# A two-layer hybrid decoder trunk: 28 of 32 tiles of the first feed-forward product, in pairs, by seven products of half blocks in place of eight

## The chip, the cores and the metric

One core of one Trainium2 chip runs the whole program. The metric is device time in microseconds (us): 1336.36 us, the median of three runs (1335.64 to 1336.46).

## The reference, cut to what matters

Two layers over 512 tokens of width 1024, all in fp32. Each layer has one input projection, four token mixers beside each other (a gated delta rule, latent attention, HGRN2, dilated attention), one output projection, and a feed-forward block, with a layer norm behind each half:

```
for l in range(2):
    h = x @ w_in[l]                                   # 1024 -> about 3100
    mixed = concat(A(h), B(h), C(h), D(h)) @ w_out[l]
    x = layer_norm(alpha * x + mixed, ln1_g[l], ln1_b[l])
    x = layer_norm(alpha * x + square(relu(x @ w_ff1[l])) @ w_ff2[l], ln2_g[l], ln2_b[l])
```

The product `x @ w_ff1[l]` is 512 by 1024 by 4096, and `... @ w_ff2[l]` is 512 by 4096 by 1024.

## The kernel before, in words

Every large product is made of three matmuls in the fp32r type: an operand is split into a high part (the value rounded to fp32r, written by ScalarE) and a low part (the value less its high part, written by VectorE), and `mm3` adds high by high, high by low and low by high in PSUM. For a weight tile of 128 by 1024 the raw tile is `wr` (loaded by a DMA that SyncE issues, two buffers), its parts are `wh` and `wl` (five buffers each). `weights` loads and splits, `split` is the pair of instructions. The stream x stands transposed, as `xH` and `xL`, eight blocks of 128 channels by 512 tokens.

The first feed-forward product goes tile by tile. A tile is 128 of the 4096 outputs: `proj` runs eight channel blocks by three matmuls, 24 matmuls of 512 columns, into one PSUM buffer; then ScalarE writes relu into `h2` and VectorE multiplies it by the PSUM value, which squares it. The first four tiles run as two halves of 256 columns (tokens 256 to 511 first), so that they can begin while the layer norm still makes the other tokens; the other 28 are full width. The second product then takes the 32 tiles `h2` as its weights side: each is split into `hH` and `hL`, and 24 matmuls of 512 columns per tile add into eight PSUM buffers.

`layer_norm(0, ...)` ends the first half of a layer: it normalises four blocks of 128 tokens without scale and bias into `xt`, transposes them on TensorE, and applies scale and bias on the way out of PSUM (`lny`), from which `xH` and `xL` are split. The residual needs the same values untransposed: before, `flush` loads scale and bias as tables (`ln`), multiplies and adds (16 VectorE instructions) early in the first feed-forward product, and writes the result to memory (`mid`); `load_x` fetches it 12 tiles before the end of the second product.

The order is not that of the text. Each instruction is recorded with its dependencies (class `Plan`), and `order` chooses at build time, by table costs, which goes next on which engine; `BIAS`, `FILL`, `EMA` and the counts of buffers steer it. Each engine then works strictly in the order that came out. Nearly every instruction passes through the one line that calls the engine (L522 before, L523 in the changed file), so rows are told apart by the tile's name. Rows from the trace drop buffer numbers, and write `h` for `h2`.

Of the kernel before, what the change touches and what calls it, by code (L numbers as in the profile page):

```python
# [9 lines left out]
FT = mybir.dt.float32  # L10
FR = mybir.dt.float32r
I32 = mybir.dt.int32
AF = mybir.ActivationFunctionType
OP = mybir.AluOpType
# [13 lines left out]
           "cf0", "cf1", "cq0", "cq1", "ci0", "ci1", "cg0", "cg1",  # L28
           "bq", "bkv", "dk0", "dk1", "dq0", "dq1", "dva", "dvb"]
ROWS = 41  # L30
BIGS = 5
RESERVE = {"row": 0, "ps": 0}
FIFO = ("wr", "wh", "wl")
FILL = (0.1, 0.4)
EMA = 3000.0
BURST = 4
PATIENCE = 1000.0
DENSE = 0.8
BIAS = {('', 've'): -550, ('A', 'ac'): 400, ('A', 'po'): 1400, ('A', 've'): -25, ('A0', 'ac'): -250,
# [4 lines left out]
GROUPS = ((2, 3), (4, 5), (0, 1, 6, 7))  # L44
WBIAS = 0
OBIAS = 400
# [117 lines left out]
class Plan:  # L164
# [48 lines left out]
    def cost(self, e, method, out, ins, k):  # L213
        n = math.prod(out.shape[1:])
        psum = any(v.buf.kind == "ps" for v in [out, *ins])
        if e == "pe":
            if method == "transpose":
                return 109.0
            w, x = k["lhsT"], k["rhs"]
            n, m = math.prod(x.shape[1:]), w.shape[1]  # L220
            if w.dt == FR:
                return max(n * 0.4167 + 13.5, 109.0)
            t = 2 * max(2 * n * 0.4167 + 3, 2 * min(m, n) * 0.4167 + 3, 25.0)
            return t
        if e == "ve":
            if method == "transpose":
                wide = len(out.shape) > 2 and out.shape[1] == 8
                return 446.0 if wide else 1045.0
            if method in ("tensor_scalar", "tensor_copy") and not psum:
                return 64 + 0.52 * n  # L230
            if method == "memset":
                return 30.0
            if method == "reciprocal":
                return 68 + 6.3 * n
            if method == "scalar_tensor_tensor" and not psum and n > 64:
                return 95 + 1.1 * n
            if method == "tensor_tensor_reduce":
                return 195 + 1.045 * n
            return 67 + 1.045 * n
        if e == "ac":  # L240
            if method == "dma_start":
                return 60.0
            ap = sum(not isinstance(k.get(w, 0.0), (int, float)) for w in ("bias", "scale"))
            acc = 90.0 if k.get("accum_out") is not None else 0.0
            return (51 if psum else 93) + (60 * ap if n <= 128 and psum else 93 * ap) + acc + 0.833 * n
        if e == "po":
            if method == "tensor_scalar":
                return 150 + 4.2 * n
            return 190 + 2.2 * n
        return 450.0  # L250
# [274 lines left out]
def emit(ctx, tc, io, layers=DEPTH):  # L525
# [18 lines left out]
    def ps(tag, shape=(128, 512), name=None):  # L544
        return plan.tile("ps", list(shape), FT, tag, "mm" if tag == "mm" else None)
# [42 lines left out]
    xH = const("xH", [128, KT, S], FR)  # L588
    xL = const("xL", [128, KT, S], FR)
    xt = None  # L590
    undone, undone_tables = [], []
    xsrc = io["x"]

    def split(h, lo, src):
        ac.activation(h, src, AF.Copy)
        ve.tensor_tensor(lo, src, h.bitcast(FT), OP.subtract)

    def weights(src, bias=WBIAS, n=1024, kind="wr"):
        plan.bias = -bias
        raw = plan.tile(kind, [128, 1024], FT, "wr")[:, :n]  # L600
        sy.dma_start(raw, src)
        h = plan.tile("wh", [128, 1024], FR, "wh")[:, :n]
        lo = plan.tile("wl", [128, 1024], FR, "wl")[:, :n]
        split(h, lo, raw)
        plan.bias = 0
        return h, lo
# [6 lines left out]
    def proj(w, out, cols=slice(0, S)):  # L613
        for k in range(KT):
            ks = slice(128 * k, 128 * k + 128)
            mm3(out[:, cols], (w[0][:, ks], w[1][:, ks]), (xH[:, k, cols], xL[:, k, cols]), k == 0, k == KT - 1)
# [52 lines left out]
    for l in range(layers):  # L669
        pcol = lambda i, r=slice(0, 128): par[r, l, i:i + 1]  # L670
        wcol = lambda n: weights(io["w_in"][l, W_AT[n]])

        mixH, mixL = [None] * KT, [None] * KT
        mid = plan.tile("dram", [NT, 128, D], FT, "x1")

        def gated(ot, gate, gain, k, tag):
            sq = row("gsq")
            ac.activation(sq, ot, AF.Square)
            s = ps(tag)
            total(s, bdr, [sq])  # L680
            rsqrt(sq, s, 1.0 / 64)
            ve.scalar_tensor_tensor(sq, sq, pcol(gain), gate, op0=OP.mult, op1=OP.mult)
            m = row("gm")
            ve.tensor_tensor(m, ot, sq, OP.mult)
            mixH[k], mixL[k] = row(f"mixH{k}", FR), row(f"mixL{k}", FR)
            split(mixH[k], mixL[k], m)

        def norm_tables(i, gate, l=l):
            g = []
# [8 lines left out]
        def layer_norm(i, m, acc, scale, after, gb_=None):  # L698
# [23 lines left out]
            for c in range(2):  # L722
                cs = slice(512 * c, 512 * c + 512)
                if last:
                    ve.scalar_tensor_tensor(t[c], t[c], s[:, 5:6], gb_[1][c], op0=OP.mult, op1=OP.add)
                    sy.dma_start(after[m, :, cs], t[c])
                    continue
                ve.tensor_scalar(t[c], t[c], s[:, 2:3], s[:, 5:6], op0=OP.add, op1=OP.mult)
                o = ps("a", (128, 4, 128))
                y = row("lny")  # L730
                for j in range(4):
                    k = 4 * c + j
                    pe.transpose(o[:, j], t[c][:, 128 * j:128 * j + 128], ident)
                for j in range(4):
                    k, js = 4 * c + j, slice(128 * j, 128 * j + 128)
                    g, b = pcol(P_LN + 16 * i + k), pcol(P_LN + 16 * i + 8 + k)
                    if j in LN_ACT:
                        ac.activation(y[:, js], o[:, j], AF.Identity, bias=b, scale=g)
                    else:
                        ve.tensor_scalar(y[:, js], o[:, j], g, b, op0=OP.mult, op1=OP.add)  # L740
                ks, ms = slice(4 * c, 4 * c + 4), slice(128 * m, 128 * m + 128)
                split(xH[:, ks, ms], xL[:, ks, ms], v3(y, 4))
            if not last:
                undone.append((t, after[m]))

        def tables_of(i, f=norm_tables):
            undone_tables.append(lambda gate: f(i, gate))
# [11 lines left out]
            undone.clear()  # L759

        def load_x(gate):
            nonlocal xt
            xt = [[row("xt") for c in range(2)] for m in range(NT)]
            for m in range(NT):
                for c in range(2):
                    sy.dma_start(xt[m][c], xsrc[m, :, 512 * c:512 * c + 512], after=gate)

        def w_tile(ks, ws, m, first, last=False):
            ms, acc = slice(128 * m, 128 * m + 128), []
# [543 lines left out]
        plan.stream = "O"  # L1313
        for g in GROUPS:
            w_out(g, g is GROUPS[0], g is GROUPS[-1])
        tables_of(0)


        plan.stream = "F"

        h2 = []
        for f0 in range(0, MF, 4):
            ws = [weights(io["w_ff1"][l, f0 + i]) for i in range(4)] if f0 == 0 else None
            if f0 == 0:
                accs = [ps(t) for t in ("mm", "mm", "a", "b")]
                for cols in (slice(256, 512), slice(0, 256)):
                    for i in range(4):
                        proj(ws[i], accs[i], cols)
            if f0 == 4:
                flush()  # L1330
            for i in range(4):
                if f0 == 0:
                    o = accs[i]
                else:
                    w = weights(io["w_ff1"][l, f0 + i])
                    o = ps("mm")
                    proj(w, o)
                t = row("h2")
                ac.activation(t, o, AF.Relu)
                ve.tensor_tensor(t, t, o, OP.mult)  # L1340
                h2.append(t)
        acc = [[ps("a"), ps("a")], [ps("a"), ps("b")], [ps("b"), ps("b")], [ps("mm"), ps("mm")]]
        TAIL = 4

# [7 lines left out]
        tail, gb_ = [], None  # L1352
        xsrc = mid
        for k in range(MF):
            if k == MF - 12:
                load_x(plan.mark())
                if l == layers - 1:
                    gb_ = norm_tables(1, plan.mark())
            w = weights(io["w_ff2"][l, k])
            hk = (row("hH", FR), row("hL", FR))  # L1360
            split(hk[0], hk[1], h2[k])
            if k < MF - TAIL:
                for m in range(NT):
                    ff2(m, k, hk, w)
            else:
                tail.append((k, hk, w))
# [135 lines left out]
```

## Time and profile before

| | |
|---|---|
| median of three runs | 1336.36 us |
| profiled execution, its own time | 1334.89 us |
| span of its instructions | 1333.1 us |
| TensorE matmuls busy | 1305.4 us, 98% |
| VectorE busy | 741.6 us, 56% |
| ScalarE busy | 620.8 us, 47% |
| mean granted TensorE clock | 0.996 |
| first feed-forward product, full-width tiles | 333.4 to 490.2 us, 994.6 to 1151.4 us |
| second feed-forward product | from 490.2 us, and from 1151.4 us |

A span is the time from the first instruction to the last. The profiled execution took 1.8 us more than its span, and 1.5 us less than the median of the runs. Matmuls overlap in the engine's pipeline, so the recorded length of one is longer than the distance from its start to the next start; for a run of them the chain of waits gives the true pace.

### The profile page before, as it was taken

To read this page: it belongs to the slowest core of one execution; us is meant where nothing else is said; L and a number is where in the kernel's file an instruction comes from. 1 tells how busy PE (TensorE), PEld (TensorE's weight loads), DVE (VectorE), ACT (ScalarE), POOL (GpSimd) and SP (SyncE) were. 2 spreads that over 40 slices of the span, in tenths; PEclk is the share of its full clock that TensorE was granted. 3 is DMA by queue.
4 is the path that set the end of the run, shared out by engine and by line. 5 is a ranking of instruction groups with operands and counts; after the bars stand their busy time and mean duration, and the time that the engine had idled before them with its cause. 6 is when DMAs were issued, how large, how long until landed. Compare 5 with 4: busy or idle time off the path is not lost.

```text
span 1333.1 us, 21834 instructions
## 1 busy us (share of the span) xinstructions
PE 1305.4 (98%) x8920; PEld 1060.9 (80%) x8920; DVE 741.6 (56%) x1505; ACT 620.8 (47%) x1194; POOL 4.8 (0%) x12
## 2 busy tenths in 40 slices
PE   8999999999999999999999999999999999999997
PEld 7767778779888888888887677787898888888886
DVE  6895575666733334422479977766766333343226
ACT  6854567737322223321587545766463222333222
POOL 0000000000000000000000000000000000000000
PEclk9999999999999999999999999999999999999999
DMA  6312102323533233334132241122145323333441
GB/s 226 124 59 65 59 18 79 109 83 95 189 109 92 94 88 100 104 104 149 48 111 96 79 144 50 34 96 96 64 124 192 91 91 95 91 98 106 145 124 63
DMA packets 44163, 132.65 MB, mean 100 GB/s; under 512 B 4896, under 2 KB 5152, under 8 KB 44064
## 3 DMA queue, kind: packets, MB, share of 16 engines
q1 hardware_dynamic: 44064, 131.27, 31.3%
q8 instruction: 70, 1.15, 0.3%
q14 instruction: 29, 0.24, 0.1%
HBM read 122.86 MB, written 8.39 MB: 98 GB/s over the span
## 4 chain that ended last, share of the span: by engine, by line
PE 82%; DVE 8%; ACT 7%; issue 1%; DMA 1%; DVEq 0%; SPq 0%; ACTq 0%
PE mm L522 47%; PE a L522 19%; PE b L522 15%; ACT lny L522 2%; DVE xt L522 2%; PE o L522 1%; ACT wh L522 1%; DVE wl L522 1%; DVE U L522 1%; ACT scr L522 1%; ACT xH L522 1%; DVE T L522 1%; DMA ln<-in_ln_dram 0%; DVE sn L522 0%; ACT kt L522 0%
## 5 line engine op out<-in xcount | busy, mean ns | idle before, releaser
L522 DVE TENSOR_TENSOR wl<-wr,wh 128x1024 fp32r<-128x1024 f32 (+1 forms) x195 | 236.7, 1218 | 340.5 <-ACT wh L522 338.0
L522 ACT ACTIVATE wh<-wr 128x1024 fp32r<-128x1024 f32 (+1 forms) x195 | 204.7, 1053 | 410.3 <-PE mm L522 391.6
L522 PE MATMUL mm<-xH,wh 128*128 128x512 f32 (+1 forms) x832 | 328.0, 394 | 0.1
L522 PE MATMUL mm<-xH,wl 128*128 128x512 f32 (+1 forms) x832 | 326.2, 393 | 0.0
L522 PE MATMUL mm<-xL,wh 128*128 128x512 f32 (+1 forms) x832 | 323.4, 389 | 0.0
L522 PEld LDWEIGHTS mm<-xH,wl 128*128 128x128 f32 x832 | 156.4, 188 | 36.9 <-issue 2.9
L522 PEld LDWEIGHTS mm<-xH,wh 128*128 128x128 f32 x832 | 156.3, 188 | 34.1 <-issue 2.3
L522 PEld LDWEIGHTS mm<-xL,wh 128*128 128x128 f32 x832 | 156.2, 188 | 33.8 <-issue 1.5
L522 DVE TENSOR_TENSOR hL<-h,hH 128x512 fp32r<-128x512 f32 x64 | 43.9, 692 | 73.3 <-PE mm L522 70.6
L522 ACT ACTIVATE hH<-h 128x512 fp32r<-128x512 f32 x64 | 40.5, 632 | 93.4 <-PE mm L522 73.7
L522 PE MATMUL b<-wh,hH 128*128 128x512 f32 x192 | 74.9, 390 | 0.0
L522 PE MATMUL b<-wh,hL 128*128 128x512 f32 x192 | 74.7, 389 | 0.0
L522 PE MATMUL a<-wh,hL 128*128 128x512 f32 x192 | 74.7, 389 | 0.0
L522 PE MATMUL a<-wl,hH 128*128 128x512 f32 x192 | 74.7, 389 | 0.0
L522 PE MATMUL a<-wh,hH 128*128 128x512 f32 x192 | 74.7, 389 | 0.0
L522 PE MATMUL b<-wl,hH 128*128 128x512 f32 x192 | 74.7, 389 | 0.0
L522 PE MATMUL mm<-wh,hH 128*128 128x512 f32 x128 | 49.9, 390 | 0.0
L522 PE MATMUL mm<-wh,hL 128*128 128x512 f32 x128 | 49.8, 389 | 0.0
L522 PE MATMUL mm<-wl,hH 128*128 128x512 f32 x128 | 49.8, 389 | 0.0
L522 ACT ACTIVATE at<-at,as 128x512 f32<-128x512 f32 (+3 forms) x64 | 35.7, 559 | 21.4 <-DVE as L522 21.3
L522 DVE TENSOR_TENSOR h<-h,mm 128x512 f32<-128x512 f32 x60 | 40.9, 682 | 5.6 <-ACT h L522 5.6
L522 PEld LDWEIGHTS a<-wh,hH 128*128 128x128 f32 x192 | 36.0, 188 | 7.6
(303 smaller groups left out, 2140.1 us busy)
## 6 DMA issues: line engine op xcount, KB each, us to landing
wr<-in_w_ff_dram SPq DMA_DIRECT2D x128, 512.0 KB, 3.6
wr<-in_w_in_dram SPq DMA_DIRECT2D x47, 512.0 KB, 3.7
wr<-in_w_out_dram SPq DMA_DIRECT2D x16, 512.0 KB, 3.6
x<-xt SPq DMA_DIRECT2D x24, 256.0 KB, 2.1
xt<-x SPq DMA_DIRECT2D x24, 256.0 KB, 5.5
ln<-in_ln_dram SPq DMA_DIRECT2D x16, 256.0 KB, 5.7
x<-in_xT_dram SPq DMA_DIRECT2D x8, 256.0 KB, 5.9
dtab<-in_tabs_dram SPq DMA_DIRECT2D x8, 256.0 KB, 4.5
```

Of the source, the lines that this page charges most:

```text
L522: getattr(e.real, method)(*[real(v) for v in a], **{n: real(v) for n, v in k.items()})
```

## The change

The 28 full-width tiles become 14 pairs of tiles. Write the channels as two halves (near, far) and the tokens as two halves (early: 256 to 511, late: 0 to 255). A pair of output tiles is then a two-by-two product of blocks, which takes eight block products, or, by Winograd's form of Strassen's scheme, seven block products and a number of additions of blocks. One block product (`part`) is four channel blocks by three matmuls of 256 columns, 12 matmuls.

Three of the seven products need combinations of x (`xd`, made once in a layer from the four pairs of `lny` that `normed` keeps; a fourth combination overwrites `xH` and `xL` of the near channels and late tokens), and three need combinations of the two raw weight tiles (`wd`, made for each pair). The products are then combined out of PSUM (`u`, `v`) into the two `h2` tiles, and relu and square are two ScalarE instructions. The first four tiles stay plain.

Beside that, the scale and bias of the first norm are no longer applied in `flush` during the first product. The normalised `xt` goes to memory as it is, and `load_x` loads two wide tables and does the 16 multiplications and additions on VectorE, late in the second product. The last norm's tables become two wide loads, there is one more `big` buffer, and the planner's numbers differ.

```diff
-BIGS = 5
+LOAD = 12
+BIGS = 6
+PLAIN = 4
-FILL = (0.1, 0.4)
-EMA = 3000.0
+FILL = (0.1, 0.2)
+EMA = 2000.0
-BIAS = {('', 've'): -550, ('A', 'ac'): 400, ('A', 'po'): 1400, ('A', 've'): -25, ('A0', 'ac'): -250,
...
+BIAS = {('A', 'ac'): 425, ('A0', 'ac'): -600, ('A0', 've'): 25, ('A1', 'ac'): 225, ('A1', 'pe'): -1775,
...
+        def wide_tables(i, gate, l=l):
+            g = []
+            for t in range(2):
+                b = big("ln", (128, 2, 512))
...
                 ve.tensor_scalar(t[c], t[c], s[:, 2:3], s[:, 5:6], op0=OP.add, op1=OP.mult)
+                if not i:
+                    sy.dma_start(after[m, :, cs], t[c])
...
+            if pending is not None:
+                g, pending = pending(gate), None
+                for m in range(NT):
+                    for c in range(2):
+                        ve.tensor_tensor(xt[m][c], xt[m][c], g[0][c], OP.mult)
+                        ve.tensor_tensor(xt[m][c], xt[m][c], g[1][c], OP.add)
...
-            if f0 == 4:
-                flush()
-            for i in range(4):
-                if f0 == 0:
-                    o = accs[i]
-                else:
-                    w = weights(io["w_ff1"][l, f0 + i])
-                    o = ps("mm")
-                    proj(w, o)
-                t = row("h2")
-                ac.activation(t, o, AF.Relu)
-                ve.tensor_tensor(t, t, o, OP.mult)
-                h2.append(t)
...
+        xd = [[plan.tile("big", [128, 4, 256], FR, "xd") for _ in range(2)] for _ in range(3)]
+        xd.append([xH[:, near, late], xL[:, near, late]])
+        for j in range(2):
+            t = [row("t") for _ in range(4)]
+            ve.tensor_tensor(t[0], normed[j, 0], normed[2 + j, 0], OP.subtract)
+            ve.tensor_tensor(t[1], normed[j, 1], t[0], OP.subtract)
+            ve.tensor_tensor(t[2], normed[j, 1], normed[j, 0], OP.subtract)
+            ve.tensor_tensor(t[3], normed[2 + j, 1], t[1], OP.subtract)
+            js = slice(128 * j, 128 * j + 128)
+            for (h, lo_), d in zip(xd, t):
+                split(h[:, :, js], lo_[:, :, js], v3(d, 4))
+
+        def part(w, c, x):
+            o = ps("mm", (128, 256))
+            for k in range(4):
+                ks = slice(c + 128 * k, c + 128 * k + 128)
+                mm3(o, (w[0][:, ks], w[1][:, ks]), (x[0][:, k], x[1][:, k]), k == 0, k == 3)
+            return o
...
+        for f0 in range(PLAIN, MF, 2):
+            r0, r1 = raw(f0), raw(f0 + 1)
+            w1, wd1, wd2 = hl(), hl(), hl()
+            w22 = row("w22", FR), row("w22", FR)
...
+            split(*w1, r0)
+            wd = [row("wd") for _ in range(4)]
+            ve.tensor_tensor(wd[0], r1[:, a], r1[:, b], OP.add)
+            split(wd1[0][:, a], wd1[1][:, a], wd[0])
+            ve.tensor_tensor(wd[1], wd[0], r0[:, a], OP.subtract)
+            split(wd1[0][:, b], wd1[1][:, b], wd[1])
+            ve.tensor_tensor(wd[2], r0[:, a], r1[:, a], OP.subtract)
+            split(wd2[0][:, a], wd2[1][:, a], wd[2])
+            ve.tensor_tensor(wd[3], r0[:, b], wd[1], OP.subtract)
+            split(wd2[0][:, b], wd2[1][:, b], wd[3])
+            split(*w22, r1[:, b])
...
+            o = part(w1, 0, x11)
+            ac.activation(u[:, 0], o, AF.Copy)
+            o = part(wd1, 512, xd[1])
+            ve.tensor_tensor(u[:, 1], u[:, 0], o, OP.add)
+            o = part(w1, 512, x21)
+            ve.tensor_tensor(t0[:, early], u[:, 0], o, OP.add)
+            o = part(wd1, 0, xd[0])
+            ve.tensor_tensor(v, u[:, 1], o, OP.add)
+            o = part(wd2, 0, xd[2])
+            ve.tensor_tensor(t1[:, late], v, o, OP.add)
+            ve.tensor_tensor(t1[:, early], u[:, 1], o, OP.add)
+            o = part(wd2, 512, x22)
+            ve.tensor_tensor(t0[:, late], v, o, OP.add)
+            ac.activation(t0, t0, AF.Relu)
+            ac.activation(t0, t0, AF.Square)
+            o = part(w22, 0, xd[3])
+            ve.tensor_tensor(t1[:, early], t1[:, early], o, OP.add)
+            ac.activation(t1, t1, AF.Relu)
+            ac.activation(t1, t1, AF.Square)
```

First place: VectorE in the middle of the first product, layer 0. Before, a low part of a weight tile (`wl`) and a square (`h2`) take turns:

```order
L522 TENSOR_TENSOR wl_4456<-wr_4397,wh_4446 128x1024
L522 TENSOR_TENSOR h2_4454<-h2_4454,mm_4414 128x512
L522 TENSOR_TENSOR wl_4490<-wr_4431,wh_4480 128x1024
L522 TENSOR_TENSOR h2_4488<-h2_4488,mm_4448 128x512
L522 TENSOR_TENSOR wl_4524<-wr_4465,wh_4514 128x1024
L522 TENSOR_TENSOR h2_4522<-h2_4522,mm_4482 128x512
```

Now, on VectorE again, 12 of the 17 instructions of a pair (the pair of the raw tiles `wr_4589` and `wr_4608`; `wl_4655`, `wl_4696` and `wl_4723` are low parts of its weights, `mm_4612`, `mm_4643` and `mm_4663` products of the pair ahead of it):

```order
L523 TENSOR_TENSOR h2_4646<-u_4593,mm_4612 128x256
L523 TENSOR_TENSOR wl_4655<-wr_4589,wh_4640 128x1024
L523 TENSOR_TENSOR h2_4614<-v_4636,mm_4643 128x256
L523 TENSOR_TENSOR wd_4673<-wr_4608 128x512
L523 TENSOR_TENSOR wd_4682<-wr_4589,wr_4608 128x512
L523 TENSOR_TENSOR h2_4646<-h2_4646,mm_4663 128x256
L523 TENSOR_TENSOR wl_4696<-wd_4673,wh_4685 128x512
L523 TENSOR_TENSOR wd_4705<-wd_4673,wr_4589 128x512
L523 TENSOR_TENSOR w22_4714<-wr_4608,w22_4661 128x512
L523 TENSOR_TENSOR wl_4723<-wd_4682,wh_4708 128x512
L523 TENSOR_TENSOR wd_4735<-wr_4589,wd_4705 128x512
L523 TENSOR_TENSOR wl_4696<-wd_4705,wh_4685 128x512
```

Four instructions for two tiles have become 17, and those that take a product out of PSUM stand between those that prepare the next pair's weights.

Second place: TensorE, the same stage. Before, a tile runs through its 24 matmuls without a change of the output:

```order
L522 MATMUL mm_4482<-xH_106,wh_4344 128x512
L522 MATMUL mm_4482<-xL_110,wh_4344 128x512
L522 MATMUL mm_4482<-xH_106,wl_4354 128x512
L522 MATMUL mm_4482<-xH_106,wh_4344 128x512
L522 MATMUL mm_4482<-xL_110,wh_4344 128x512
L522 MATMUL mm_4482<-xH_106,wl_4354 128x512
```

Now, on TensorE, the part of that pair in which the second half of `wl_4696` is used (`mm_4725` and `mm_4738` need the two halves of `wd1`, `mm_4751` the first half of `wd2`):

```order
L523 MATMUL mm_4738<-xd_3756,wh_4685 128x256
L523 MATMUL mm_4738<-xd_3794,wh_4685 128x256
L523 MATMUL mm_4725<-xd_3744,wh_4685 128x256
L523 MATMUL mm_4725<-xd_3783,wh_4685 128x256
L523 MATMUL mm_4725<-xd_3744,wl_4696 128x256
L523 MATMUL mm_4725<-xd_3744,wh_4685 128x256
L523 MATMUL mm_4725<-xd_3783,wh_4685 128x256
L523 MATMUL mm_4725<-xd_3744,wl_4696 128x256
L523 MATMUL mm_4751<-xd_3764,wh_4708 128x256
L523 MATMUL mm_4751<-xd_3803,wh_4708 128x256
L523 MATMUL mm_4751<-xd_3764,wl_4723 128x256
L523 MATMUL mm_4738<-xd_3756,wl_4696 128x256
```

The product `mm_4738` is begun, left for nine matmuls of two others, and then goes on with its first matmul that needs the low part; in all a pair is 84 matmuls of 256 columns.

Third place: VectorE and the first norm's tables. Before, at the first full-width tiles of the first product:

```order
L522 TENSOR_TENSOR wl_3968<-wr_3905,wh_3960 128x1024
L522 TENSOR_TENSOR hL_3983<-h2_3951,hH_3972 128x512
L522 TENSOR_TENSOR xt_3311<-xt_3311,ln_3970 128x512
L522 TENSOR_TENSOR xt_3302<-xt_3302,ln_3970 128x512
L522 TENSOR_TENSOR xt_3315<-xt_3315,ln_3976 128x512
```

Now, on VectorE, between the weight tiles of the second product:

```order
L523 TENSOR_TENSOR wl_6687<-wr_6629,wh_6676 128x1024
L523 TENSOR_TENSOR wl_6731<-wr_6659,wh_6724 128x1024
L523 TENSOR_TENSOR xt_6674<-xt_6674,ln_6710 128x512
L523 TENSOR_TENSOR xt_6680<-xt_6680,ln_6710 128x512
L523 TENSOR_TENSOR xt_6684<-xt_6684,ln_6710 128x512
```

The 16 instructions have moved from the first product to the second, behind the low part of its tile 25.

## Rows read from the trace of the kernel before

**Rows 1.** The page: busy time and instructions of each engine; the chain's shares

```profile
PE 1305.4 (98%) x8920; PEld 1060.9 (80%) x8920; DVE 741.6 (56%) x1505; ACT 620.8 (47%) x1194; POOL 4.8 (0%) x12
...
PE 82%; DVE 8%; ACT 7%; issue 1%; DMA 1%; DVEq 0%; SPq 0%; ACTq 0%
```

**Rows 2.** Windows: length, busy PE, PEld, DVE, ACT, POOL; clock, DMA, GB/s

```profile
90.00:205.00 115.00, 111.53 (x1751) 86.35 (x1749) 77.40 (x204) 63.16 (x149) 1.85 (x2) 1.00 0.18 55
317.00:333.00 16.00, 16.00 (x134) 15.96 (x135) 8.78 (x12) 10.11 (x19) 0.00 (x0) 1.00 0.44 132
333.00:490.00 157.00, 157.00 (x676) 126.39 (x675) 64.67 (x78) 46.63 (x62) 0.00 (x0) 1.00 0.38 118
490.00:640.00 150.00, 150.00 (x664) 124.16 (x663) 51.16 (x54) 44.04 (x53) 0.00 (x0) 1.00 0.36 109
```

**Rows 3.** The chain in order of time: start, length, what

```profile
316.38 0.55 DVE xt L522
316.94 0.04 issue
316.98 2.07 PE a L522 x16
321.93 5.76 PE mm L522 x48
...
333.44 156.80 PE mm L522 x672
...
492.31 2.04 PE b L522 x9
...
994.60 156.80 PE mm L522 x672
```

**Rows 4.** Waits in 334 to 490 us: total, times, longest

```profile
ACT wh L522 <- PE mm L522: 93.9, 24, 4.1
DVE wl L522 <- ACT wh L522: 84.0, 25, 3.8
```

**Rows 5.** VectorE in order of time: start, length, what; back to back

```profile
339.91 9.12 DVE L522 TENSOR_TENSOR xt<-xt,ln 128x512 f32<-128x512 f32 x15 [3.02 <-DMA ln<-in_ln_dram]
...
350.14 0.69 DVE L522 TENSOR_TENSOR h<-h,mm 128x512 f32<-128x512 f32 x1
350.74 2.36 DVE L522 TENSOR_TENSOR wl<-wr,wh 128x1024 fp32r<-128x1024 f32 x2
...
159.03 0.43 DVE L522 TENSOR_TENSOR qa<-qa,f 128x256 f32<-128x256 f32 x1
159.37 0.42 DVE L522 TENSOR_TENSOR kr<-kr,f 128x256 f32<-128x256 f32 x1
```

**Rows 6.** Groups by form, whole span: ScalarE (count | busy, mean ns | idle)

```profile
L522 ACT ACTIVATE hH<-h 128x512 fp32r<-128x512 f32 x64 | 40.5, 632 | 93.4 <-PE mm L522 73.7 <-DVE h L522 14.2 <-DVE hL L522 5.3
...
L522 ACT ACTIVATE tt<-b 128x256 f32<-128x256 f32 x16 | 5.7, 388 | 0.1
```

**Rows 7.** One weight tile on its way: ScalarE, VectorE, SyncE's next issue

```profile
378.05 1.06 ACT L522 ACTIVATE wh<-wr 128x1024 fp32r<-128x1024 f32 x1 [4.00 <-PE mm L522]
379.14 1.23 DVE L522 TENSOR_TENSOR wl<-wr,wh 128x1024 fp32r<-128x1024 f32 x1 [3.73 <-ACT wh L522]
380.39 0.33 SPq L522 DMA_DIRECT2D wr<-in_w_ff_dram  x1
```

**Rows 8.** The tile `wr`, 300 to 480 us: from issue to landing

```profile
DMA to landing us min/median/max: 3.3/3.6/6.8
```

**Rows 9.** From the last matmul of a PSUM tile to VectorE

```profile
304.34 0.39 PE L522 MATMUL o<-wh,mixL 128*128 128x512 f32 x1
304.77 0.69 DVE L522 SCALAR_TENSOR_TENSOR xt<-xt,o 128x512 f32<-128x512 f32 x1 [0.23 <-PE o L522]
```

**Rows 10.** Groups by form, 310 to 334 us: matmuls of 256 columns, weight loads

```profile
L522 PE MATMUL mm<-xL,wh 128*128 128x256 f32 x29 | 8.2, 283 | 0.0
...
L522 PEld LDWEIGHTS mm<-xH,wl 128*128 128x128 f32 x30 | 5.7, 189 | 0.0
```

More of the change, by code (lines that the diff above doesn't have):

```diff
@@ L221, in cost @@
             if w.dt == FR:
-                return max(n * 0.4167 + 13.5, 109.0)
+                return max(n * 0.4167 + (20 if n > 256 and x.buf.name in ("xH", "xL") else 13.3), 109.0)
             t = 2 * max(2 * n * 0.4167 + 3, 2 * min(m, n) * 0.4167 + 3, 25.0)
@@ L590, in emit @@
     xt = None
-    undone, undone_tables = [], []
+    undone, undone_tables, pending = [], [], None
     xsrc = io["x"]
@@ L673, in emit @@
         mixH, mixL = [None] * KT, [None] * KT
+        normed = {}
         mid = plan.tile("dram", [NT, 128, D], FT, "x1")
@@ L686, in gated @@
             split(mixH[k], mixL[k], m)
+        def wide_tables(i, gate, l=l):
+            g = []
+            for t in range(2):
+                b = big("ln", (128, 2, 512))
+                src = io["ln"]
+                sy.dma_start(b, bass.AP(tensor=src.tensor, ap=[[0, 128], [512, 2], [1, 512]],
+                                        offset=src.offset + ((l * 2 + i) * 2 + t) * D), after=gate)
+                g.append([b[:, 0], b[:, 1]])
+            return g
         def norm_tables(i, gate, l=l):
@@ L742, in layer_norm @@
                 split(xH[:, ks, ms], xL[:, ks, ms], v3(y, 4))
-            if not last:
+                normed[m, c] = y
+            if not last and i:
                 undone.append((t, after[m]))
@@ L761, in load_x @@
         def load_x(gate):
-            nonlocal xt
+            nonlocal xt, pending
             xt = [[row("xt") for c in range(2)] for m in range(NT)]
@@ L1315, in emit @@
             w_out(g, g is GROUPS[0], g is GROUPS[-1])
-        tables_of(0)
+        pending = lambda gate, f=wide_tables: f(0, gate)
         plan.stream = "F"
         h2 = []
-        for f0 in range(0, MF, 4):
-            ws = [weights(io["w_ff1"][l, f0 + i]) for i in range(4)] if f0 == 0 else None
-            if f0 == 0:
-                accs = [ps(t) for t in ("mm", "mm", "a", "b")]
-                for cols in (slice(256, 512), slice(0, 256)):
-                    for i in range(4):
-                        proj(ws[i], accs[i], cols)
-            if f0 == 4:
-                flush()
-            for i in range(4):
-                if f0 == 0:
-                    o = accs[i]
-                else:
-                    w = weights(io["w_ff1"][l, f0 + i])
-                    o = ps("mm")
-                    proj(w, o)
-                t = row("h2")
-                ac.activation(t, o, AF.Relu)
-                ve.tensor_tensor(t, t, o, OP.mult)
-                h2.append(t)
+        early, late = slice(256, 512), slice(0, 256)
@@ new lines, in emit @@
+        ws = [weights(io["w_ff1"][l, f]) for f in range(PLAIN)]
+        accs = [ps(t) for t in ("mm", "mm", "a", "b")]
+        for cols in (early, late):
+            for w, o in zip(ws, accs):
+                proj(w, o, cols)
+        for o in accs:
+            t = row("h2")
+            ac.activation(t, o, AF.Relu)
+            ve.tensor_tensor(t, t, o, OP.mult)
+            h2.append(t)
+        near, far = slice(0, 4), slice(4, 8)
+        xd = [[plan.tile("big", [128, 4, 256], FR, "xd") for _ in range(2)] for _ in range(3)]
@@ new lines, in part, with raw @@
+        def part(w, c, x):
[4 more added lines that the diff above has]
+            return o
+        def raw(f):
+            r = plan.tile("wr", [128, 1024], FT, "wr")
+            sy.dma_start(r, io["w_ff1"][l, f])
+            return r
+        hl = lambda: (plan.tile("wh", [128, 1024], FR, "wh"), plan.tile("wl", [128, 1024], FR, "wl"))
@@ new lines, in emit @@
+        x11, x21, x22 = ([t[:, ks, cs] for t in (xH, xL)] for ks, cs in ((near, early), (far, early), (far, late)))
+        for f0 in range(PLAIN, MF, 2):
+            r0, r1 = raw(f0), raw(f0 + 1)
+            w1, wd1, wd2 = hl(), hl(), hl()
+            w22 = row("w22", FR), row("w22", FR)
+            a, b = slice(0, 512), slice(512, 1024)
+            split(*w1, r0)
[9 more added lines that the diff above has]
+            split(*w22, r1[:, b])
+            t0, t1 = row("h2"), row("h2")
+            u = row("u", shape=(128, 2, 256))
+            v = row("v", shape=(128, 256))
+            o = part(w1, 0, x11)
[17 more added lines that the diff above has]
+            ac.activation(t1, t1, AF.Square)
+            h2 += [t0, t1]
@@ L1354, in emit @@
         for k in range(MF):
-            if k == MF - 12:
+            if k == MF - LOAD:
                 load_x(plan.mark())
                 if l == layers - 1:
-                    gb_ = norm_tables(1, plan.mark())
+                    gb_ = wide_tables(1, plan.mark())
             w = weights(io["w_ff2"][l, k])
```

7 rows, old and new, of the table BIAS are left out of this document.

## The prediction, made before the changed kernel had run

> **What bounds the kernel now.** I read the page's first part, then the chain of waits, the windows, the waits and, for durations, the groups and the order of time. TensorE is busy 98% of the span and 82% of the chain; the other engines stand at 56% and 47% [rows 1]. That alone says little, since recorded matmuls overlap. The chain says more: both first products are one unbroken run of 672 matmuls in 156.80 us [rows 3], with TensorE busy for the whole window at clock 1.00 [rows 2]. The waits there run one way: ScalarE waits for TensorE 93.9 us, VectorE for ScalarE 84.0 us [rows 4], and nothing of note waits for a load. So a shorter matmul list shortens the stage, for as long as the others keep up.
>
> **TensorE, taken away and added.** A full-width tile is 24 matmuls; 28 tiles are the 672. Their pace is 156.80 / 672 = 233.3 ns, 11.20 us for two tiles. A pair is now 7 x 12 = 84 matmuls of 256 columns. The chain has 48 of exactly this shape in 5.76 us [rows 3]: 120.0 ns each. A pair then takes 10.08 us, 14 pairs 141.1 us, against 156.8 us: 15.7 us less in a layer, 31.4 us in two. Seven eighths would be 39.2 us; the rest goes because two matmuls of 256 take 240.0 ns where one of 512 takes 233.3 ns. The new operand `xd` isn't in the trace; I give it the 120.0 ns of `xH`, and as its other end 113.4 ns, half the 226.7 ns of a matmul of the second product (9 in 2.04 us [rows 3]), on three products of seven: 36 x 6.6 ns x 28 = 6.7 us better.
>
> That a halved matmul must not wait for its weights is seen in the same run: each recorded weight load is 189 ns [rows 10], and PEld is busy 15.96 of 16.00 us in the window of the halves against 126.39 of 157.00 in full width [rows 2], yet the pace is 120.0 ns, so loads overlap. The Trainium skill (TensorE: Matmul & The Clock Gate, "Back-to-back issue gap") gives an isolated matmul N / 2.4 ns and about 2.5 more, some 109 and 216 ns here; by that the saving would be (48 x 0.216 - 84 x 0.109) x 28, about 34 us, by its estimate. The rows, 120.0 and 233.3 ns, decide.
>
> **VectorE, added.** Two tiles had four instructions; a pair has 17: one low part of 1024, five of 512, four sums of raw weights of 512, seven of 256 that take products out of PSUM. Back to back, fifteen of 512 take 9.12 us, so 602 ns from start to start with 0.69 recorded; two of 1024 take 2.36 us, so 1.13; those of 256 start 0.334 apart, and one of 512 that reads PSUM is followed after 0.60 [rows 5]. Sum: 1.13 + 9 x 0.602 + 7 x 0.334 = 8.89 us in 10.08 us, 88%. It fits, but what hid VectorE's work (92 us of idle in 157) is nearly gone. With no overlap, by recorded lengths [rows 5, 7], it would be 1.23 + 9 x 0.69 + 7 x 0.42 = 10.4 us.
>
> Here a rule speaks against the change. Recorded lengths are longer than the distance between starts in every row of 5. The Trainium skill (VectorE: DVE Perf Modes, "The DRAIN you can't avoid") says that the next instruction doesn't start until the pipeline of the one before is empty. By the rows it does start, some 0.09 us before the recorded end; the rule's case is a rival below.
>
> **ScalarE, added.** One of 1024, nine of 512, one of 256 out of PSUM, by recorded lengths 1.06 + 9 x 0.63 + 0.39 = 7.1 us a pair of 10.08 [rows 6, 7]: hidden.
>
> **Waits that are new: two circuits.** A pair's period is also that of each circle of waits, which averages don't show.
> (A) The two raw buffers. Once `w22` has read the second raw tile, SyncE issues the next load 0.02 us later [rows 7] and it lands in 3.6 us [rows 8]; `wh` takes 1.06 us, `wl` starts 0.03 us on [rows 7]; then VectorE's order up to the next `w22`: 1.13, two of 256, two of 512 between them, then low part, sum, `w22`. That is 0.02 + 3.6 + 0.03 + 1.06 + 0.03 + 1.13 + 0.67 + 4 x 0.602 + 0.69 = 9.64 us: 0.44 us to spare.
> (B) Through TensorE. `mm_4612`'s last matmul is followed by VectorE two of 256, one of 1024, one of 256, two of 512, one of 256, six of 512, up to the low part that `mm_4738` waits for; then TensorE has 19 matmuls to the end of the like product. From the last matmul to VectorE: 0.43 us from the start at 512 columns, of which 0.39 is the matmul's recorded length [rows 9]; at 256 its length is 0.28 [rows 10], so 0.32, which is 0.20 past the next slot. VectorE to TensorE: 0.04 us behind the recorded end [rows 3]. Sum: 0.20 + 0.67 + 1.13 + 0.33 + 1.20 + 0.33 + 3.61 + 0.09 + 0.04 + 2.28 = 9.88 us: 0.20 us to spare. Behind the waiting low part stand the next product's reads, and all of VectorE follows.
> Both are under 10.08, so TensorE stays the bound, narrowly.
>
> **The start of the stage.** VectorE has 16 instructions of 512 more (eight differences, eight low parts), 9.6 us. From the last transposes (316.98) to the first full-width matmul (333.44) TensorE has 16.5 us [rows 3], and VectorE was busy 8.78 of 16 us there [rows 2]. So the first pairs run with VectorE late; walking the first pairs by the durations above, I find one wait of about 0.35 us in the fourth pair. I count 0.4 us a layer, 0.8 us in all, with ends at 0 and 3 us a layer.
>
> **The moved tables.** Sixteen instructions, 9.8 us, go into a window where VectorE is busy 51.16 of 150 us [rows 2]. Behind them wait low parts of later tiles; five buffers of `wh` and `wl` keep up to four tiles ready, 4 x 5.44 us of TensorE work, against about 10 us of loads and 9.6 us of instructions. Cost nothing; without that cover the difference beyond it, at most some 5 us a layer. The writes of the normalised `xt` come earlier on SyncE's queue, ahead of loads not due for a pair: nothing.
>
> **The mixers.** The planner's numbers reorder all mixers. TensorE is idle 27.7 us in the whole span [rows 1], 3.5 us in a mixer window of 115 [rows 2]. I take nothing, with ends of 8 us better and 10 us worse.
>
> **Sum.** 1334.9 (the profiled execution) - 31.4 + 0.8 = 1304.3; the median stood 1.5 above, so 1306 us, a span of 1302 to 1303.
>
> **The rivals.**
> 1. VectorE sets the pair. For it: 88% and only 0.20 us to spare in circuit B. If none of its 13 instructions there overlapped, 12 x 0.09 makes 10.9 us a pair: only 0.3 x 28 = 8 us is saved, 1328 us; if hops are longer by 0.05 each, 10.1 to 10.2, 1308 to 1310 us. Against it: fifteen in a row at 602 ns, and the same out of PSUM.
> 2. The loads set it, and the kernel is slower. Circuit A is 6.04 us plus the time to landing. Above 4.04 us it costs; at 5.16 us a pair is the old 11.2 us; at the longest seen, 6.8 us [rows 8], 12.84 us, so 1.64 x 28 = 46 us slower, 1382 us. For it: two loads are asked for within some 1.3 us of each other in each pair, where before they came evenly. Against it: the median of 3.6 us, and DMA engines busy 0.38 of the stage [rows 2], which the same weights in 10.08 in place of 11.20 us raise to about 0.42.
> 3. The mixers' new order costs 10 to 15 us, and the gain is halved: 1316 to 1321 us. For it: many small waits there; against: the same instructions, idle time small before.
> 4. The matmuls of `xd` run at 113.4 ns, or the mixers gain: 1297 to 1300 us.
>
> **How the numbers follow.** Forecast 0.66; rival 1, 0.12; rival 2, 0.07 (part of it short of 5.16 us and still faster); rival 3, 0.09; rival 4, 0.06. The measurement can tell 0.2%, 2.7 us. Slower: most of rival 2 and a little of 3, 0.06; the same 0.04; faster 0.90. The range for 8 in 10, from 1297 to 1320, takes in rival 4, the mild form of 1 and the nearer part of 3; beyond lie the hard forms of 1 and 2.
>
> **What would show it.** In the profile after: runs of matmuls of 256 columns at 120 ns in the first product, the stage from the first product with `xd` to the second product near 141 us, VectorE busy near 0.88 in it; few waits of TensorE for `wl`; `wr` landing in about 3.6 us; the second product still 2.04 us for nine matmuls; mixers within some us. I am wrong if the stage takes over 145 us, if TensorE waits for `wl` in each pair, or if the mixers move by more than 10 us.

## The result, and the profile after

The changed kernel takes 1303.87 us, the median of four runs (1303.22 to 1305.55), against 1336.05 us (four runs, one more than stood in the table above; 1335.64 to 1336.46) of the kernel before: a ratio of 0.9761, 95% interval 0.9744 to 0.9778. The forecast was 1306 us, with a range of 1297 to 1320. The profiled execution took 1303.82 us, its span 1302.0 us.

The page's first line after, to be set beside [rows 1]:

```profile
PE 1274.4 (98%) x9928; PEld 1088.7 (84%) x9928; DVE 913.2 (70%) x1901; ACT 719.7 (55%) x1406; POOL 4.8 (0%) x12
```

TensorE has 1008 matmuls more, as counted, and is busy 31 us less. VectorE is 172 us busier and ScalarE 99 us, and none of that shows in the time.

The chain of waits after, in order of time (start, length, what), which answers to [rows 3]:

```profile
331.96 67.63 PE mm L523 x564
...
406.41 5.94 DMA wr<-in_w_ff_dram
...
416.70 13.83 PE mm L523 x113
...
437.35 5.97 DMA wr<-in_w_ff_dram
...
447.68 26.73 PE mm L523 x221
474.41 2.05 PE a L523 x9
476.46 2.04 PE b L523 x9
...
626.74 8.16 PE a L523 x36
...
979.30 140.98 PE mm L523 x1176
1120.28 2.06 PE a L523 x9
```

In layer 1 all 14 pairs are one unbroken run: 1176 matmuls in 140.98 us, 119.9 ns each. In layer 0 the run is cut twice by a load that took 6 us, and the stage takes 474.41 - 331.96 = 142.45 us. The second product is as it was, 2.04 us for nine.

So the 31.1 us of the span come about like this, by the starts of stages in both chains: pairs of layer 0, 14.4 us; pairs of layer 1, 15.8 us; the part ahead of layer 0's pairs, 1.5 us (333.44 to 331.96); between layer 0's second product and layer 1's first, 0.5 us lost; the rest, nothing. The 1.5 us can't be called the change's doing: kernels 4, 9 and 12 below have the changed kernel's order of instructions up to there (9 and 12 with fewer small buffers), and their chains reach layer 0's pairs at 333.38, 332.92 and 334.68 us, on both sides of the 333.44 us of the kernel before. The 0.5 us is smaller than that scatter.

The windows after, to be set beside [rows 2] (length, busy PE, PEld, DVE, ACT, POOL; clock, DMA share, GB/s):

```profile
316.00:332.00 16.00, 16.00 (x136) 15.96 (x135) 15.98 (x26) 13.05 (x27) 0.00 (x0) 1.00 0.30 82
332.00:474.40 142.40, 141.44 (x1177) 141.03 (x1176) 125.65 (x234) 86.77 (x150) 0.95 (x1) 1.00 0.31 103
474.40:627.00 152.60, 152.60 (x675) 126.35 (x674) 66.44 (x77) 49.35 (x63) 0.96 (x1) 1.00 0.41 131
979.30:1120.20 140.90, 140.90 (x1178) 140.90 (x1177) 126.05 (x236) 88.36 (x152) 0.00 (x0) 1.00 0.32 104
```

VectorE is busy 126.05 of 140.90 us in the pairs, 89%, where 88% was worked out; ahead of them it is busy without a gap, 15.98 of 16.00. TensorE's granted clock is 1.00 in all four windows. In the second product VectorE is 15 us busier (66.44 against 51.16 us, in a stretch 2.6 us longer); the tables' 16 instructions are 9.8 us of that, the rest are splits of weights and of `h2` that fall into this window. TensorE has no gap there.

### The profile page after: what moved, and what is told of

Same layout as the page of the kernel before. It is cut to its first block, busy times and chain, and to the rows that moved or that the text cites. A ratio compares the mean times of both kernels' runs of the same rounds, so it can differ in the third digit from the quotient of the medians.

```text
span 1302.0 us, 24504 instructions
## 1 busy us (share of the span) xinstructions
PE 1274.4 (98%) x9928; PEld 1088.7 (84%) x9928; DVE 913.2 (70%) x1901; ACT 719.7 (55%) x1406; POOL 4.8 (0%) x12
## 4 chain that ended last, share of the span: by engine, by line
PE 76%; DVE 12%; ACT 9%; issue 2%; DMA 1%; DVEq 0%; SPq 0%; ACTq 0%
PE mm L523 41%; PE a L523 19%; PE b L523 15%; ACT lny L523 2%; DVE wl L523 1%; ACT wh L523 1%; DVE xt L523 1%; PE o L523 1%; DMA wr<-in_w_ff_dram 1%; ACT scr L523 1%; DVE U L523 1%; ACT xH L523 1%; DVE T L523 1%; DVE X L523 1%; DVE dt L523 0%
## 5 line engine op out<-in xcount | busy, mean ns | idle before, releaser
L523 ACT ACTIVATE wh<-wr 128x1024 fp32r<-128x1024 f32 (+1 forms) x167 | 175.5, 1055 | 322.0 <-PE mm L523 233.3
L523 PE MATMUL mm<-xH,wh 128*128 128x256 f32 (+1 forms) x720 | 244.1, 340 | 0.1
L523 PE MATMUL mm<-xH,wl 128*128 128x256 f32 (+1 forms) x720 | 243.5, 339 | 0.0
L523 PE MATMUL mm<-xL,wh 128*128 128x256 f32 (+1 forms) x720 | 243.0, 337 | 0.0
L523 PE MATMUL mm<-xd,wh 128*128 128x256 f32 x672 | 121.8, 283 | 1.0 <-ACT wh L523 1.0
L523 PEld LDWEIGHTS mm<-xd,wh 128*128 128x128 f32 x672 | 103.7, 191 | 1.4 <-ACT wh L523 1.4
L523 PE MATMUL mm<-xd,wl 128*128 128x256 f32 x336 | 91.7, 283 | 0.0
L523 ACT ACTIVATE wh<-wd 128x512 fp32r<-128x512 f32 x112 | 69.6, 625 | 15.1 <-DVE wd L523 14.7
L523 DVE TENSOR_TENSOR wl<-wd,wh 128x512 fp32r<-128x512 f32 x112 | 76.1, 686 | 0.2
L523 ACT ACTIVATE h<-h 128x512 f32<-128x512 f32 x112 | 67.4, 620 | 13.9 <-DVE h L523 13.6
L523 PEld LDWEIGHTS mm<-xd,wl 128*128 128x128 f32 x336 | 63.1, 192 | 0.0
```

Source lines behind the costliest of these rows:

```text
L523: getattr(e.real, method)(*[real(v) for v in a], **{n: real(v) for n, v in k.items()})
```

## The experiments

Twelve kernels ran. Each ratio is to the kernel before on the same chip. Its median was 1336.45 to 1336.99 us beside the experiments, so differences from the changed kernel's 1303.87 us, which are given below in us, are good to about 1 us.

### 1. The pairs undone, the rest kept

```diff
-        for f0 in range(PLAIN, MF, 2):
...
+        for f in range(PLAIN, MF):
+            w = weights(io["w_ff1"][l, f])
+            o = ps("mm")
+            proj(w, o)
```

> The changed kernel with its pairs undone: all 32 tiles plain, the 28 at full width; the moved tables and the planner's new numbers stay. Theory (the gain is TensorE's time in the pairs): the first product is 156.8 us again in each layer, and with the mixers' small gain of 0.9 us seen in the trace after, the time is 1335 us (1333 to 1337). Rival (the planner's numbers and the moved tables carry a good part of the gain): under 1328 us.

Measured: 1335.5 us, ratio 0.9991 (0.9982 to 1.0). The stage is 156.80 us for 672 matmuls again in both layers. The planner's new numbers and the moved tables together are worth about 1 us where there are no pairs (0.9 us; the interval reaches from nothing to 2.4), so the gain needs the pairs.

### 2. Halves without the scheme

```diff
-            proj(w, o)
+            proj(w, o, early)
+            proj(w, o, late)
```

> As the kernel with all tiles plain, but the 28 tiles run as two halves of 256 columns each, eight half-block products in place of seven, without sums. Theory (a matmul of 256 columns is 120.0 ns, one of 512 in this product 233.3): 28 x 24 x 6.7 ns = 4.5 us more in a layer, 9.0 us in two, 1344 us. Rival (the time goes by columns, so that halving is free and seven eighths is the whole account): 1335 us.

Measured: 1345.23 us, ratio 1.0058 (1.0039 to 1.0077), 9.7 us above the kernel with full-width tiles. Its chain, where the first product is one run in each layer:

```profile
333.68 161.28 PE mm L523 x1344
...
999.84 161.28 PE mm L523 x1344
```

161.28 / 1344 is 120.0 ns, with `xH` alone, so halving costs 4.48 us a layer, and 9.0 of the 9.7 us. Seven products of halves are 7 x 12 x 0.120; at this pace the full eighth is not to be had with matmuls of 256 columns.

### 3 and 4. The same 0.60 us of VectorE in two places

The order is fixed first; then one instruction of a pair is issued a second time, in experiment 3 the first sum of raw weights, in experiment 4 the last low part.

```diff
+            plan.twice.add(plan.mark())     # behind wd[0] = r1[a] + r1[b], or behind the split of wd[3]
```

> The changed kernel with the first sum of raw weights (wd[0]) issued twice on VectorE in each pair, every engine's order else the same: 0.60 us more per pair, inside the circuit from the product mm_4612's like to the low part that TensorE waits for. Theory (the circuit counts): 9.88 + 0.60 = 10.48 us a pair, 0.40 x 28 = 11 us slower, 1315 us (1311 to 1318). Rival (VectorE's sum counts): 8.89 + 0.60 = 9.49 us, under 10.08, so 1304 to 1305 us.

> The changed kernel with the low part of the last half of wd2 issued twice on VectorE in each pair, every engine's order else the same: the same 0.60 us more per pair, but behind the circuit's last instruction, ahead of the sum u, where VectorE waits 0.7 to 0.9 us for TensorE in the trace after. Theory: hidden, 1304 to 1306 us. Rival (any added VectorE time in a pair counts at this load): 1310 us or more.

Measured: with the sum 1322.75 us (ratio 0.9888, 0.9866 to 0.9911), 18.9 us above the changed kernel; with the low part 1306.98 us (0.977, 0.9749 to 0.979), 3.1 us above it. The second is a little more than I expected, and not all of it is the pairs' own, as the chain shows (starts of the pairs and of the second product, layer by layer):

```profile
333.38 33.79 PE mm L525 x282
...
476.17 2.05 PE a L525 x9
...
980.99 18.70 PE mm L525 x156
...
1123.58 2.06 PE a L525 x9
```

The pairs take 142.79 and 142.59 us, where the changed kernel has 142.45 and 140.98: 2.0 us more, nearly all of it in layer 1; in this profiled execution 1.4 us more were lost ahead of the first pair (333.38 against 331.96), where both kernels run the same instructions in the same order. So the same busy time costs about six times as much in one place as in the other, and by the pairs alone still more: a pair's waits go by the circuit and not by VectorE's sum. But 18.9 us is more than the 11 expected, 0.67 us a pair. One period of the chain of the kernel with the doubled sum shows where my circuit was wrong:

```profile
404.26 3.88 PE mm L525 x30
...
408.92 1.14 DVE wl L525
410.05 0.33 DVE h L525
410.38 0.61 DVE wd L525
410.99 0.02 issue
411.02 0.70 DVE wd L525
411.72 0.02 issue
411.74 0.63 ACT wh L525
412.38 1.04 ACT h L525 x2
413.42 0.53 ACT wh L525
413.94 0.52 ACT h L525
414.46 0.53 ACT wh L525
414.99 0.04 issue
415.03 3.88 PE mm L525 x30
```

The period is 415.03 - 404.26 = 10.77 us. TensorE waits for a high part (`wh`, ScalarE), not for the low part: behind the sum ScalarE has a high part, two instructions on `h2`, another high part and one more on `h2` ahead of the last high part, strictly in order. In the changed kernel the same circuit ends like this (layer 1, ScalarE, then TensorE's run that begins with that high part's product):

```profile
1049.81 0.63 ACT L523 ACTIVATE wh<-wd 128x512 fp32r<-128x512 f32 x1
...
1052.43 0.62 ACT L523 ACTIVATE wh<-wd 128x512 fp32r<-128x512 f32 x1
...
1053.22 0.64 PE L523 MATMUL mm<-xd,wh 128*128 128x256 f32 x4
```

The high part is done at 1053.05, 0.04 us of way make 1053.09, and the matmul is due at 1053.22: 0.13 us to spare, less than the 0.20 I had found by way of `wl`. The circuit is then 9.95 us. The doubled sum adds 0.72 us, not 0.60, since the second write of the same tile waits for the first and starts only behind its recorded end (0.61, 0.02, 0.70), and TensorE's run takes 0.1 us longer when it has to start anew (408.14 - 404.26 = 3.88 where 29 starts of 0.12 and one length of 0.28 make 3.76; the trace has the 0.1 us in the first four starts, from 404.26 to 404.84): 9.95 + 0.72 + 0.1 = 10.77 us.

### 5 and 9. A third raw buffer

```diff
-WRS = 2
+WRS = 3
```

Experiment 5 does just this (with 40 row buffers in place of 41, for room) and lets the planner order anew. Experiment 9 orders with two and hands out three when the order is fixed (with fewer small buffers, for room).

> The changed kernel with three raw weight buffers in place of two (and 40 row buffers in place of 41, for room): the next pair's loads no longer wait for this pair's last read of both raw tiles. Theory (the 1.5 us that layer 0's pairs lost, 142.5 us against 141.0 in layer 1, came from two loads that took 6 us to land): both layers' pairs at 141.0 to 141.3 us, 1301 to 1304 us with the mixers' order a little changed. Rival (the loss came from VectorE or ScalarE): layer 0 still near 142.5 us.

> The changed kernel in its own order on every engine, instruction for instruction, with a third raw weight buffer given out when the order is already fixed (and fewer small buffers, for room). Theory: the two waits of layer 0's pairs go and nothing else moves, pairs 141.0 us in both layers, 1302.4 us (1301 to 1304). Rival (the third buffer itself made the kernel with 40 row buffers 12 us slower): 1312 us or more.

Measured: 1316.05 us (ratio 0.986, 0.984 to 0.9879) and 1303.19 us (0.9756, 0.974 to 0.9772). The chain of experiment 5 at the pairs, and then that of experiment 9:

```profile
344.43 140.93 PE mm L523 x1176
...
992.12 140.94 PE mm L523 x1176
```

```profile
332.92 140.98 PE mm L524 x1176
...
977.90 141.14 PE mm L524 x1176
```

In both, layer 0's pairs are unbroken now, so its 1.5 us came from the two loads. Loads of 6 us are there in experiment 9 too (6.39 and 6.02 us in layer 0), and with the third buffer they cut nothing. Experiment 5 loses 12 us for another reason: its pairs of layer 0 begin at 344.43 us, 12.5 us later, since another count of buffers gave the mixers another order. That is rival 3 of the prediction, met in another kernel. Experiment 9 has the best median of all, but 0.7 us below the changed kernel is within what these runs scatter; a gain is not shown.

### 6. The tables left in the first product

```diff
...
-        pending = lambda gate, f=wide_tables: f(0, gate)
+        tables_of(0)
...
+            if f0 == PLAIN + 2:
+                flush()
```

> The changed kernel without the second part of the change: the first norm's scale and bias are applied by 16 VectorE instructions (9.6 us) in the first product again, after its first pair. Theory (VectorE has 1.2 us to spare in a pair, the circuit 0.1 to 0.2): some 4 to 9 us of waits in each layer's first pairs, 1312 to 1322 us. Rival (the move of the tables is of no account): 1304 to 1306 us.

Measured: 1327.83 us, ratio 0.995 (0.9933 to 0.9967), 24 us above the changed kernel and beyond the 1312 to 1322 us that I expected. The chain in layer 0:

```profile
345.26 6.19 DMA ln<-in_ln_dram
351.44 0.02 issue
351.47 1.32 DVE xt L523 x3
...
353.88 6.70 DVE xt L523 x11
...
364.98 120.44 PE mm L523 x982
```

VectorE waits in order for the tables, then spends its 9.6 us on them, and TensorE stands 8.5 us in one piece for a high part. I had counted the instructions and not the landing. Nor had I counted the clock. One window behind the stand shows it (length, busy time of the engines; clock, DMA share, GB/s):

```profile
365.00:370.00 5.00, 5.00 (x23) 4.98 (x24) 3.81 (x8) 2.54 (x4) 0.00 (x0) 0.50 0.63 210
```

TensorE's granted clock, 1.00 before the stand, is 0.50 here, that is 1.2 GHz in place of 2.4: 23 matmuls in 5 us, where about 42 fit at 0.120. The run of 982 behind the stand takes 120.44 us in place of 117.8. Layer 1 has a like stand and loses 1.7 us behind it, so that some 4 of the 21.7 us by which this profiled execution is longer are the clock's. In this place and order the scheme without the move keeps a fourth of the gain: the second part of the change does not save time, it clears VectorE for the first.

### 7 and 8. Two plain tiles, or eight

```diff
-PLAIN = 4
+PLAIN = 2     # or 8, the added four at full width
```

> The changed kernel with 2 plain tiles in place of 4, so 15 pairs in a layer. Theory of the price alone: a pair saves 11.20 - 10.08 = 1.12 us, with tiles of the halved kind 11.52 - 10.08 = 1.44 us, so 2.9 us less in two layers, 1301 us. Rival (VectorE, busy 15.98 of 16 us ahead of the first pair already, is late for it): waits of 2 to 8 us a layer at the start, 1304 to 1317 us.

> The changed kernel with 8 plain tiles in place of 4 (the added four at full width), so 12 pairs in a layer. Theory: 2 x 2 x 1.12 = 4.5 us slower, 1308 us (1307 to 1310). Rival (each pair costs more than the 10.08 us, by waits that the last pairs' look hides): under 1307 us.

Measured: 1309.21 us with two (ratio 0.9807, 0.9788 to 0.9826), 5 us worse; 1307.09 us with eight (0.979, 0.9772 to 0.9809), 3.2 us worse. With two, VectorE is late, as the rival said, and layer 0's chain leads through its `xd` and `wl` to two loads asked for late, of which the second took 5.77 us. With eight, the 28 tiles behind the first four are one unbroken run in both layers (1104 matmuls in 143.19 and 143.20 us; 96 x 233.3 + 1008 x 119.9 ns is 143.3); layer 1 loses the 2.2 us of two pairs, and layer 0 less, because its run isn't cut by slow loads. That makes the loss a little less than the 4.5 us expected.

### 10. The planner's numbers of before

```diff
-FILL = (0.1, 0.2)
-EMA = 2000.0
+FILL = (0.1, 0.4)
+EMA = 3000.0
...
+BIAS = {('', 've'): -550, ('A', 'ac'): 400, ('A', 'po'): 1400, ('A', 've'): -25, ('A0', 'ac'): -250,
...
```

> The changed kernel with the planner's numbers of before (FILL, EMA, BIAS): pairs and moved tables stay. Theory (the new numbers are worth 0.9 us or so in the mixers, and the pairs bring the rest): 1303 to 1309 us. Rival (the order of the mixers carries weight of its own, as the 12 us between two orders in the kernel with 40 row buffers let suspect): 1310 us or more.

Measured: 1306.93 us, ratio 0.979 (0.9771 to 0.981), 3 us above the changed kernel, in runs that scatter from 1306.55 to 1311.11 us. With experiment 1 the numbers are worth some 1 to 3 us, little above the scatter; the pairs bring the rest.

### 11 and 12. The load doubled, with two raw buffers and with three

```diff
             r0 = raw(f0)
+            plan.twice.add(plan.mark())
             r1 = raw(f0 + 1)
```

> The changed kernel with the load of each pair's first raw tile issued twice into the same buffer, every order else the same. Theory (the circuit of the two raw buffers is 6.04 us plus the time to landing): if the second follows the first, 7.4 us to landing, 13.4 us a pair, 94 us slower, 1398 us; if they overlap, 5.3 us, 11.3 us a pair, 36 us slower, 1340 us. Rival (loads are hidden): 1304 to 1307 us.

> The same doubled load with the third raw buffer, which opens the circuit: the load can start a buffer earlier, about half a pair, 5 us. Theory: most of the loss of the doubled load with two buffers goes, 1303 to 1320 us. Rival (the queue or the bytes are the bound, not the buffers): within 10 us of the doubled load with two buffers.

Measured: 1390.51 us with two (ratio 1.0408, 1.039 to 1.0425), 1304.76 us with three (0.9768, 0.9753 to 0.9784). One period of the chain with two buffers:

```profile
398.97 1.07 ACT wh L525
...
405.02 3.53 DMA wr<-in_w_ff_dram
408.56 0.02 issue
408.57 3.64 DMA wr<-in_w_ff_dram
412.21 0.02 issue
412.23 1.06 ACT wh L525
```

The second load into the same tile waits for the first, 7.2 us in all, and the pair takes 412.23 - 398.97 = 13.26 us. My circuit A gives 6.04 + 7.2 = 13.24. This is rival 2 in full, made by hand, and it is slower than the kernel before. The third buffer opens the circuit, and the doubled load, with a megabyte and a half a pair in place of one, costs nothing that can be told: it was the two buffers and not the bytes.

## Why the prediction was right

- **TensorE's pace.** Right: 119.9 ns for 1176 matmuls, with `xd` no different from `xH`, so the end at 113.4 ns is out. Undisturbed, a layer saves 15.8 us (expected 15.7).
- **Cover of VectorE and ScalarE.** Right in size (89% against 88%). (Four of the seven products use sums of the raw weights, not three as the section on the change has it; the count of 17 instructions holds all four.) The rule of the Trainium skill that spoke against it (VectorE: DVE Perf Modes, "The DRAIN you can't avoid"), that an instruction starts when the one before is through, was read too widely: the same section adds that an instruction that is not held back starts earlier. Taken for all instructions it would have put a pair at 10.4 us or more; the trace disagrees, layer 1 has 10.07. In the trace an instruction starts behind the recorded end of the one before where it depends on it and waits for a semaphore: the doubled sum, 0.02 us behind (experiment 3), and in the changed kernel `v`, which reads `u` (1046.33 behind 1046.29).
- **Circuit A.** Right, to 0.02 us, by experiment 11. The longest landing, 6.8 us, was priced in rival 2, but for every pair; that single loads take 6 us was left out of the sum: twice in layer 0, 1.5 us together, which experiments 5 and 9 took away. There the load is the pair's second; ScalarE waits for it in order, and the high parts stand behind.
- **Circuit B.** The mechanism was right and the route wrong: the last link is ScalarE's high part, 0.13 us to spare where I had 0.20 by the low part. It changed nothing in the sum, since both are under 10.08 us, but experiment 3 came out 8 us above what I expected.
- **The start of the stage.** Wrong in size: I counted 0.8 us for waits in the fourth pair, and there were none in either layer. The 16.5 us of plain halves covered it, though barely: with half as many plain tiles it is late (experiment 7).
- **The moved tables.** Right: no gap in the second product.
- **The mixers.** Taken as nothing. In the one profiled execution the part ahead of layer 0's pairs was 1.5 us shorter and the part between the layers 0.5 longer, which is within what kernels with the same order differ by. That this is a small number is no rule: another order cost 12 us (experiment 5).

The sum was 31.4 - 0.8 = 30.6 us; it came as 31.6 for the pairs, less 1.5 for the two loads, and 1.0 more outside the pairs, 31.1 us of span. The mechanism is right, but that the sum comes within half a microsecond is luck: the waits at the start that didn't come (0.8), the loads that did (1.5) and a microsecond of scatter nearly cancel.

## What to carry to other kernels

When TensorE is the bound, price a scheme of fewer products by a run of exactly the smaller matmul, since its overhead takes part of the eighth (here 31.6 of 39.2 us came through). Then write down each circle of waits, with every instruction that stands in order behind the waiting one, on ScalarE too, and compare its length with TensorE's period: in experiments 3 and 4 the place inside the circle was dear and the one outside nearly free, at the same busy shares. A scheme that loads the other engines to nine tenths needs them cleared of other work first, as experiment 6 shows. A spare buffer in a circle of loads can hide loads twice as long (experiments 11 and 12), though with the loads as they are its gain here is not shown.

## What the runs showed of the hardware that I had not expected

Most loads of a weight tile (512 KB) landed in 3.7 us (median after), but the two that cut layer 0's pairs took 5.94 and 5.97 us; kernels 4 and 10 have two such in layer 0 as well (5.69 and 6.19, 6.27 and 5.69 us), layer 1's pairs in these kernels were cut by none over 3.6 us. The traces show what stands beside such a load. From the DMA view of 404 to 414 us after, around the first (its busy tenths in 40 slices, and one of its queues):

```profile
DMA  0000000069497796596798421100000000000000
...
q8 instruction: 1, 0.02, 0.6%
```

From 410.5 us on the 16 DMA engines together are busy less than a tenth of the time, though the load lands only at 412.35 us, and a packet of 16 KB of the queue `q8 instruction` lies within the load. In the pairs of the changed kernel and of kernels 3 to 10 the traces have 492 loads of weight tiles, of which 42 took over 5 us; beside 40 of these a packet of that queue was under way. Of the 323 loads beside which there was no instruction packet at all, one took over 5 us (5.18). Still, 107 loads that had one beside them stayed under 5 us, and no experiment moved these packets, so that they are the cause is likely and not shown.

TensorE, once it had waited for an operand, took about 0.1 us more for its next 30 matmuls than in an unbroken run (experiment 3). And after it had stood for 8.5 us its granted clock was 0.50 (experiment 6).
